# A six-layer block on one core: gate and output products tied behind the steps of a chunk loop, products grouped by tile shape, and router work moved

## The chip, the cores and the metric

The kernel runs on one core of a Trainium2 chip. The metric is the device time of one execution in microseconds (us); the time before is the median of three runs. Five engines work side by side, each through its own instructions in order: TensorE (PE) for matrix products, VectorE (DVE), ScalarE (ACT), GpSimd (POOL), and SyncE (SP), which here issues the DMA transfers. An engine waits on semaphores that the others, or landed transfers, raise.

## The reference

512 tokens of width 1024 in fp32 pass four layers (convolution, state-space, RWKV, convolution) and then two layers of another block, each a mixer of four parts and a mixture of experts.

```python
for i in range(4):                          # first block
    y = (short_conv, s5, rwkv7, short_conv)[i](x, ...)
    r = DN_ALPHA * x + y
    r = r + (p[i] @ ple_proj[i]) * sigmoid(r @ ple_gate[i])
    x = layer_norm(r, ln_g[i], ln_b[i])
...
def rwkv7_mixer(x, ...):                    # 16 heads of 64
    r, k, v, z = einsum("nbld,nde->nble", xs[:4], w_rkvz)
    ...
    sa = einsum("bhvk,bhk->bhv", state, -kk_t)          # each token t
    state = state * w_t + sa * (kk_t * a_t) + v_t * k_t
    out_t = einsum("bhvk,bhk->bhv", state, r_t)
    out = group_norm(out) * lnx_g + lnx_b + bonus
    return (out * silu(z)) @ w_out
...
# second block, layer l = 0, 1: s, b, g come from c @ w_ada
h = rms_norm(x, norm1_g[l]) * (1 + s1) + b1
x = x + g1 * token_mixer(h, ...)            # attention, pooling, HGRN recurrence, convolution
h = rms_norm(x, norm2_g[l]) * (1 + s2) + b2
x = x + g2 * hierarchical_moe(h, router weights, ...)   # 32 experts, two per token
```

## The kernel before

Activations are kept transposed: eight tiles `xp` of 128 channels by 512 tokens. A dense product takes its weights by `L338` (an SP load of raw weights `wr`), splits them into a high half `wh` on ACT (L315) and a low half `wl` on DVE (L317), and makes three products on PE (L423): high by high, low by high and high by low. The kernel is written with tile pools, and a scheduler that models time orders each engine's instructions before they are compiled. `behind(ins)` adds to that order one edge: what is issued under it comes after `ins` on the engine of `ins`. It adds no wait at run time.

**The RWKV chain** (`rwkv_chain`) goes through eight chunks of 64 tokens, 16 heads as 8 by 2 (`order`). Each chunk has four groups of products: `p1` (L1476, 16 products with `gx`), `p2` (L1481, 16 with `ad` and `rh`), `p3` (L1488, 16 with `bt`, for the next state `nsv`) and `po` (32: L1504 on `gx` and the state `sv`, L1502 on `ad` and `sa`), with ACT and DVE copies between them. `invert` (L1447, L1454, with DVE's L1456) makes the next chunk's `ad`; `loads` fetches it (L1431, L1432, L1433, L1436, L1438, L1325). At eight places in a chunk `fill()` advances generators: `zgen`, the gate's dense products `ptp<-xs` in pieces of six, then `wout(0)`, the first half of the output's products (`ptp<-H`, 256 columns); and `norms` and `post`, which normalise the chunks (`settle`, L1387) and gate them. Nothing but the scheduler's model sets where among the steps PE does these. What is left of them is done behind the chain.

**The state-space layer** makes y (L970 with `ow` and `X`, 64x64; L968 with `tw` and `U`, 128x64) in eight blocks. **The recurrence** of the second block's mixers makes its output from `At` and `v`, and `St` and `qb`, in four blocks (two layers by two).

**Bounds and router.** `bounds()` runs at the beginning of the first mixer, called mix0. Among its loads it stores two columns of `gs` (norm gain times scale) and of `mod` of each layer into DRAM (`d_gp`, [128, 8] turned to "k p", so in pieces of one value) and reads them back in another layout (`gp`, L1595), which the first mixture of experts uses. The stores of `mod` were placed by the scheduler in the last convolution layer, those of `gs` at the start of mix0. The seam into mix0 also holds the normalisation `mixer_operand` (L1671 sums squares on POOL and DVE, L458 reduces them on PE). `moe_before(l)` loads the router's weights (L2198), scales them by `gs` into `gw` on DVE (L2200), and makes the bias `rb` (L2199, L2203 on PE, L2204). It is written in the mixer behind its operands; the scheduler placed its load and `gw` in the seam. SP's loads go out on one DMA queue, in SP's order; an instruction that waits holds those behind it.

## Time and profile before

| | us |
|---|---|
| median of three runs | 3395.87 |
| the three runs | 3387.91, 3395.87, 3414.22 |
| profiled execution | 3395.55 |
| its span in the trace | 3393.8 |
| PE busy in it | 3023.4 |

The profile is one profiled execution. Its span is the trace's length; the profiled execution's own time holds some two microseconds more. A line of a timeline gives start, duration, engine, line, operation, output and inputs, shape and count, and in brackets the idle time of the engine ahead of it and what ended that. PE's records overlap, since products are pipelined, so the time of a run is the distance from its start to the next start. In the RWKV chain each small product leaves two records (x32 is 16 products). PEld is the load of the fixed operand, which runs beside PE.

### The profile page before, as it was taken

How to read it: one execution, taken by the hardware profiler on the slowest of the kernel's cores; microseconds unless marked ns; L12 is line 12 of the kernel's file. 1: busy time of each engine (PE TensorE's matmuls, PEld its weight loads, DVE VectorE, ACT ScalarE, POOL GpSimd, SP SyncE). 2: the span in 40 equal slices, each digit the busy share in tenths (PEclk: the TensorE clock that was granted, in tenths of full speed). 3: DMA queues.
4: the chain of work that ended last, by engine and by line, in shares of the span. 5: the costliest groups of instructions: out<-in, count | busy, mean ns of one | idle time of the engine just before them, and what ended most of it. 6: DMA issues, size and time to landing. Idle time of an engine off the chain costs nothing. (4 is left out here: it accounts for less than half of the span.)

```text
span 3393.8 us, 57476 instructions
## 1 busy us (share of the span) xinstructions
PE 3023.4 (89%) x23218; PEld 2174.3 (64%) x23218; DVE 2006.5 (59%) x3911; ACT 1031.5 (30%) x1695; POOL 876.2 (26%) x738
## 2 busy tenths in 40 slices
PE   6999989988879887998699979989979996998997
PEld 5677767865557776777575656555647565655564
DVE  6754495467965678788667454544447845354443
ACT  3233324356533332222253322111125343111111
POOL 2911321125422455420305230110011523010000
PEclk9999899988887897999798779999989887999999
DMA  5453562314677545586420048999982003799997
GB/s 168 133 158 100 147 173 67 110 59 140 177 198 222 169 150 167 162 235 211 90 75 20 28 159 323 413 415 415 416 303 67 28 17 152 295 414 407 416 416 323
DMA packets 443070, 690.46 MB, mean 203 GB/s; under 512 B 68720, under 2 KB 354800, under 8 KB 408944
## 3 DMA queue, kind: packets, MB, share of 16 engines
q1 hardware_dynamic: 441648, 684.63, 58.1%
q8 instruction: 185, 3.03, 0.4%
q10 hardware_dynamic: 1152, 2.10, 0.2%
q14 instruction: 85, 0.70, 0.1%
HBM read 642.08 MB, written 46.94 MB: 203 GB/s over the span
## 5 line engine op out<-in xcount | busy, mean ns | idle before, releaser
L317 DVE TENSOR_TENSOR wl<-wr,wh 128x1024 fp32r<-128x1024 f32 (+2 forms) x275 | 324.5, 1182 | 216.8 <-ACT wh L315 98.2
L315 ACT ACTIVATE wh<-wr 128x1024 fp32r<-128x1024 f32 (+2 forms) x290 | 270.7, 939 | 542.9 <-PE pmm L423 193.8
L2400 PE MATMUL pmm<-raw,xg 128*32 128x128 f32 (+1 forms) x5120 | 348.6, 323 | 5.0 <-DMA raw<-in_w_dram 4.1
L2400 PEld LDWEIGHTS pmm<-raw,xg 128*32 128x32 f32 (+1 forms) x5120 | 226.7, 123 | 121.8 <-issue 49.5
L2545 POOL TENSOR_SCALAR Ra<-sp,cf 128x512 f32<-128x512 f32 x28 | 44.6, 1593 | 789.0 <-PE pst L2584 739.1
L423 PE MATMUL pmm<-H,wh 128*128 128x512 f32 x680 | 206.8, 414 | 9.2 <-ACT cg L2073 4.0
L423 PE MATMUL pmm<-H,wl 128*128 128x512 f32 x680 | 204.3, 408 | 2.0 <-DVE wl L317 2.0
L423 PE MATMUL pmm<-L,wh 128*128 128x512 f32 x680 | 202.4, 406 | 0.1
L2560 DVE SCALAR_TENSOR_TENSOR xp<-pst,mod,xp 128x512 f32<-128x512 f32 x196 | 142.7, 747 | 64.1 <-PE pst L2585 60.0
L2427 PE MATMUL pas<-raw,gT 128*32 128x256 f32 (+1 forms) x1472 | 165.9, 450 | 12.1 <-DVE gT L2421 11.0
L1556 DVE SCALAR_TENSOR_TENSOR war<-wa,cs,war 128x256 f32<-128x256 f32 x252 | 156.6, 637 | 3.8
L423 PEld LDWEIGHTS pmm<-H,wh 128*128 128x128 f32 x680 | 130.6, 197 | 41.7 <-ACT cg L2073 4.2
L423 PEld LDWEIGHTS pmm<-H,wl 128*128 128x128 f32 x680 | 131.5, 196 | 34.8 <-issue 3.6
L423 PEld LDWEIGHTS pmm<-L,wh 128*128 128x128 f32 x680 | 131.1, 195 | 30.6 <-issue 1.7
L2635 ACT COPY Y<-pas 32x256 f32<-32x256 f32 (+1 forms) x92 | 37.8, 411 | 288.0 <-DVE Y L2635 287.9
L2453 PE MATMUL pst<-R,hH 128*128 128x320 f32 (+4 forms) x448 | 91.9, 321 | 33.3 <-DVE R L2444 30.3
L2407 DVE TENSOR_TENSOR g<-g,pmm 128x256 f32<-128x256 f32 (+1 forms) x56 | 20.3, 362 | 167.1 <-ACT g L2406 166.8
L2427 PEld LDWEIGHTS pas<-raw,gT 128*32 128x32 f32 (+1 forms) x1472 | 59.4, 119 | 91.7 <-issue 57.9
L2635 DVE COPY Y<-pas 32x256 f32<-32x256 f32 (+1 forms) x92 | 43.7, 475 | 125.8 <-PE pas L2427 118.1
L2406 ACT ACTIVATE g<-pmm 128x256 f32<-128x256 f32 (+1 forms) x56 | 18.9, 338 | 301.1 <-PE pmm L2400 301.1
L2400 PE MATMUL pas<-raw,xg 128*32 128x128 f32 (+1 forms) x2048 | 97.3, 292 | 11.7 <-SPq L2505 6.6
L2453 PEld LDWEIGHTS pst<-R,hH 128*128 128x128 f32 x448 | 69.4, 201 | 55.2 <-DVE R L2444 35.5
(869 smaller groups left out, 6801.2 us busy)
## 6 DMA issues: line engine op xcount, KB each, us to landing
raw<-in_w_dram SPq DMA_DIRECT2D x384, 1024.0 KB, 13.4
wa<-in_w_ada_dram SPq DMA_DIRECT2D x48, 1024.0 KB, 6.6
wr<-in_conv_w_in_dram SPq DMA_DIRECT2D x64, 512.0 KB, 4.8
wr<-in_w_in_dram SPq DMA_DIRECT2D x34, 512.0 KB, 4.1
wr<-in_ple_gate_dram SPq DMA_DIRECT2D x16, 1024.0 KB, 5.4
wr<-in_rwkv_w_rkvz_dram SPq DMA_DIRECT2D x16, 1024.0 KB, 5.4
wr<-in_conv_w_out_dram SPq DMA_DIRECT2D x8, 1024.0 KB, 5.2
wr<-in_ssm_w_in_dram SPq DMA_DIRECT2D x8, 1024.0 KB, 6.2
```

The costliest lines, as they stand in the source:

```text
L315: self.nc.scalar.activation(h, x, AF.Copy)
L317: (eng or self.nc.vector).tensor_tensor(l, x, h.bitcast(FT), OP.subtract)
L423: nc.tensor.matmul(ps[i], ws[i][w][:, perm[k]], x[k], start=n == first[i], stop=n == last[i])
L1556: E.scalar_tensor_tensor(acc, w[:, k], cs[:, k:k + 1], acc, op0=OP.mult, op1=OP.add)
L2400: nc.tensor.matmul(p[c * n:c * n + n, w // 2 * W:w // 2 * W + W], x[:, j, o:o + n], ws[w][:, jj, c * W:c * W + W], start=j == 0, stop=j == 7)
L2406: nc.scalar.activation(g, p[:, 0:W], AF.Sigmoid)
L2407: nc.vector.tensor_tensor(g, g, p[:, 0:W], OP.mult)
L2427: nc.tensor.matmul(py[q * n:q * n + n, 0:W], gT[:, o:o + n], ws[4 + j // 2][:, j % 2, q * W:q * W + W], start=j == 0, stop=j == 3)
L2453: T.matmul(p[:, :n], (self.hH, self.hL)[i // 4][:, i % 4, j], R[:, i % 4, :n], start=i == 0, stop=i == 7)
L2545: G.tensor_scalar(a, P[0], s, None, op0=OP.is_equal)
L2560: self.done = self.nc.vector.scalar_tensor_tensor(self.xp[m], p, self.mod[l][:, 40 + m:41 + m], self.xp[m], op0=OP.mult, op1=OP.add).ins
L2635: (nc.scalar.copy if q % 2 else nc.vector.tensor_copy)(self.block[1][o:o + n, q * W:q * W + W], p[q * n:q * n + n])
```

## The change

Six parts. In the chain, `fill(step)` issues the dense generators (`main`) behind the last product of the step just issued, so that on PE the piece comes after that step; the gate's pieces have three products, not six; four of the gate's output tiles are made ahead of the chain; and `po` makes its 16 products of one shape, then the 16 of the other. In the state-space layer and in the recurrence the two shapes of products are grouped in the same manner. The `d_gp` stores move from `bounds()` into `moe_before(0)`, and the `gp` load to the beginning of the mixture of experts. `moe_before` is issued behind the end of the mixer's normalisation (on DVE) and behind the last weight load (on SP).

```diff
-        self.nc.sync.dma_start(raw, W[:, c0:c0 + n].rearrange("(k p) n -> p k n", p=128))
+        self.loaded = self.nc.sync.dma_start(raw, W[:, c0:c0 + n].rearrange("(k p) n -> p k n", p=128)).ins
...
-                for gg in range(4):
-                    for c in range(3):
+
+                for c in range(3):
+                    for gg in range(4):
                         for g2, r in enumerate(rs):
                             o = py[g2][r, gg * 128:(gg + 1) * 128]
                             if c == 2:
-                                nc.tensor.matmul(o, U[q][:, m % 2 * 8 + g2 * 4 + gg], tw[g2][:, gg], start=False, stop=True)
+                                nc.tensor.matmul(o, U[q][:, m % 2 * 8 + g2 * 4 + gg], tw[g2][:, gg], start=False, stop=gg == 3)
...
-        zgen = self.dense_gen(zop, A["rwkv_w_rkvz"][0][3], range(0, D, 256), z_sink, ptag="tp", piece=6,
+        zgen = self.dense_gen(zop, A["rwkv_w_rkvz"][0][3], range(0, D, 256), z_sink, ptag="tp", piece=3,
                               then=(A["rwkv_w_out"][0], 0, 256))
...
-        def fill(n=1):
-            for _ in range(n):
+        def fill(step=None):
+
+            with self.behind(step and step.ins):
                 while main and next(main[0], StopIteration) is StopIteration:
                     main.pop(0)
-                for q in (norms, norms, post):
-                    if q and next(q[0], StopIteration) is StopIteration:
-                        q.pop(0)
+            for q in (norms, norms, post):
+                if q and next(q[0], StopIteration) is StopIteration:
+                    q.pop(0)
...
         nxt = loads(0)
+
+        while len(zs) < 4:
+            fill()
         for _ in invert(nxt[1], nxt[4]):
             fill()
...
-            fill()
+            fill(step)
...
-            for h in range(8):
-                for w in range(2):
-                    for q in range(2):
-                        rd = slice(64 - q * 64, 128 - q * 64)
-                        out = po[vr[q], h * 64:h * 64 + 64]
-                        if w:
-                            T.matmul(out, ad[sr[q], h, rd], sa[q][sr[q], h], start=False, stop=True)
-                        else:
-                            T.matmul(out, gx[:, q * 8 + h, rd], sv[q][:, h], start=True, stop=False)
+
+            for w in range(2):
+                for h, q in order:
+                    rd = slice(64 - q * 64, 128 - q * 64)
+                    out = po[vr[q], h * 64:h * 64 + 64]
+                    if w:
+                        step = T.matmul(out, ad[sr[q], h, rd], sa[q][sr[q], h], start=False, stop=h == 7)
+                    else:
+                        T.matmul(out, gx[:, q * 8 + h, rd], sv[q][:, h], start=h == 0, stop=False)
...
-        d = self.dr.tile([2, 2, 8, 128], FT, name="d_gp")
-        for l in range(2):
-            nc.sync.dma_start(d[l, 0].rearrange("k p -> p k"), self.gs[l][:, 8:16])
-            nc.sync.dma_start(d[l, 1].rearrange("k p -> p k"), self.mod[l][:, 24:32])
-        nc.sync.dma_start(self.gp, d.rearrange("l i (a b) c -> l i (a b c)", a=1).rearrange("l i (p j) -> p l i j", j=8))
...
-                for c in range(4):
-                    for hh, r in enumerate(half):
-                        o = po[r, c * 128:c * 128 + 128]
-                        T.matmul(o, vt[:, c, r], At[:, c * 4 + i * 2 + hh], start=True, stop=c == 0)
-                        if c:
-                            T.matmul(o, St[r, i * 3 + c - 1], qb[i][r, c * 128:c * 128 + 128], start=False, stop=True)
+
+                for w in range(2):
+                    for c in range(w, 4):
+                        for hh, r in enumerate(half):
...
-            self.moe_before(l)
+
+            with self.behind(normed), self.behind(self.loaded):
+                self.moe_before(l)
...
+        if self.d_gp is None:
+
+            self.d_gp = d = self.dr.tile([2, 2, 8, 128], FT, name="d_gp")
+            for i in range(2):
+                nc.sync.dma_start(d[i, 0].rearrange("k p -> p k"), self.gs[i][:, 8:16])
+                nc.sync.dma_start(d[i, 1].rearrange("k p -> p k"), self.mod[i][:, 24:32])
...
+        if not l:
+            nc.sync.dma_start(self.gp, self.d_gp.rearrange("l i (a b) c -> l i (a b c)", a=1).rearrange("l i (p j) -> p l i j", j=8))
```

PE in the RWKV chain before, at the third chunk, from the end of a gate piece to the beginning of `po` (the third column is output and inputs, then the shape and a count of equal rows):

```order
L423 MATMUL ptp_8845<-xs_7588,wh_8846 128x512
L423 MATMUL ptp_8845<-xs_7587,wl_8847 128x512
L1454 MATMUL pst_8156<-ad_7946,R_8126 32x32 x16
L1481 MATMUL pmm_8247<-rh_8223,ad_7946 64x64
L1504 MATMUL pmm_8301<-sv_7962,gx_7948 64x64
L1504 MATMUL pmm_8301<-sv_7963,gx_7948 64x64
L1481 MATMUL pmm_8247<-rh_8223,ad_7946 64x64 x15
L1488 MATMUL pas_8272<-sa_7950,bt_7949 64x64
L1502 MATMUL pmm_8301<-sa_7950,ad_7946 64x64
L1488 MATMUL pas_8272<-sa_7951,bt_7949 64x64
```

and the changed kernel at the second chunk, where `p1` has become L1481, `p2` L1486 and the two kinds of `po` L1509 and L1507:

```order
L1481 MATMUL pas_8078<-sv_7861,gx_7846 64x64
L423 MATMUL ptp_7817<-xs_7573,wl_7819 128x512
L423 MATMUL ptp_7817<-xs_7580,wl_7819 128x512
L423 MATMUL ptp_7817<-xs_7587,wl_7819 128x512
L1486 MATMUL pmm_8103<-rh_8079,ad_7844 64x64 x16
L423 MATMUL ptp_8122<-xs_7538,wh_8123 128x512
L423 MATMUL ptp_8122<-xs_7545,wh_8123 128x512
L423 MATMUL ptp_8122<-xs_7552,wh_8123 128x512
L1509 MATMUL pmm_8153<-sv_7860,gx_7846 64x64
L1509 MATMUL pmm_8153<-sv_7861,gx_7846 64x64
```

Gate pieces of three now stand behind `p1` and behind `p2`, and the L1509 products that begin here are sixteen in a row.

SP at the start of mix0 before, from the stores of `gs` to the router's loads:

```order
L1593 DMA d_gp<-gs_13250 128x8x1
L1593 DMA d_gp<-gs_13253 128x8x1
L1651 DMA cf_13402<-in_constf_dram 128x1499
L1653 DMA mi_13404<-in_consti_dram 128x192
...
L338 DMA wr_13486<-in_w_in_dram 128x8x128
L2198 DMA wr_15246<-in_w_router_dram 128x8x36
L2199 DMA rb_15248<-in_rb_dram 128x36
```

and the changed kernel in the middle of mix0, from the mixer's last input weights to the first of its output weights:

```order
L338 DMA wr_14833<-in_w_in_dram 128x8x128
L2205 DMA d_gp<-gs_13250 128x8x1
L2206 DMA d_gp<-mod_78 128x8x1
L2205 DMA d_gp<-gs_13253 128x8x1
L2206 DMA d_gp<-mod_79 128x8x1
L2209 DMA wr_15245<-in_w_router_dram 128x8x36
L2210 DMA rb_15247<-in_rb_dram 128x36
L2477 DMA gp<-d_gp 128x4x8
L338 DMA wr_15493<-in_w_out_dram 128x4x256
```

The four stores have come together, ahead of the router's weights.

DVE in the seam into mix0 before, with the router's `gw` ahead of the sum of squares:

```order
L517 SCALAR_TENSOR_TENSOR xp_76<-xp_76,vec,pst_13191 128x512
L517 SCALAR_TENSOR_TENSOR xp_77<-xp_77,vec,pst_13191 128x512
L2200 TENSOR_TENSOR gw_15247<-wr_15246,gs_13250 128x288
L1671 TENSOR_TENSOR sq_13276<-sq_13276,sq_13281 128x512
L1671 TENSOR_TENSOR sq_13296<-sq_13296,sq_13298 128x512
```

and in the changed kernel, in the middle of mix0 (`hd` belongs to the recurrence, `mq` to attention):

```order
L1815 TENSOR_TENSOR hd_14187<-hd_14187,hq_13912 128x8x32
L1815 TENSOR_TENSOR hd_14242<-hd_14242,hq_13836 128x16x16
L2211 TENSOR_TENSOR gw_15246<-wr_15245,gs_13250 128x288
L2018 SCALAR_TENSOR_TENSOR mq_13683<-mq_13683,vec_13393,pas_13901 128x512
L2018 SCALAR_TENSOR_TENSOR mq_13706<-mq_13706,vec_13393,pas_13916 128x512
L1810 TENSOR_TENSOR hd_14303<-hb_13747 128x16x16
L1811 TENSOR_TENSOR hd_14303<-hb_13747 128x16x16
L317 TENSOR_TENSOR wl_14592<-wr_14346,wh_14591 128x1024
```

`gw` has moved from the seam to a place between `hd` and `mq` (there L2018, before L2015).

## Rows read from the trace of the kernel before

**Rows 1.** The page's busy time, share of the span and instructions: TensorE.

```profile
PE 3023.4 (89%) x23218; PEld 2174.3 (64%) x23218; DVE 2006.5 (59%) x3911; ACT 1031.5 (30%) x1695; POOL 876.2 (26%) x738
```

**Rows 2.** Windows of the chain: busy time by engine, granted clock, DMA share, GB/s.

```profile
1040.00:1060.00 20.00, 18.24 (x277) 14.40 (x277) 12.54 (x27) 7.68 (x14) 9.09 (x7) 1.00 0.89 283
1060.00:1080.00 20.00, 17.92 (x252) 14.58 (x248) 11.74 (x39) 4.55 (x10) 4.16 (x4) 0.50 0.81 235
...
1100.00:1120.00 20.00, 18.91 (x218) 15.81 (x218) 11.51 (x25) 6.84 (x16) 14.82 (x20) 0.55 0.62 171
1120.00:1140.00 20.00, 19.43 (x326) 16.85 (x326) 14.26 (x40) 8.84 (x15) 4.57 (x5) 1.00 0.63 161
...
1160.00:1180.00 20.00, 12.47 (x99) 10.38 (x98) 10.82 (x33) 7.73 (x16) 7.38 (x14) 0.81 0.46 144
```

**Rows 3.** Timeline of TensorE in the chain, 1055 to 1131.

```profile
1055.86 0.63 PE L423 MATMUL ptp<-xs,wh 128*128 128x512 f32 x2
...
1059.11 0.29 PE L1481 MATMUL pmm<-rh,ad 64*64 64x64 f32 x2 [1.76 <-DVE ad L1456]
...
1068.80 0.48 PE L1504 MATMUL pmm<-sv,gx 128*64 128x64 f32 x4
...
1072.09 1.06 PE L1447 MATMUL pst<-t,ad 32*32 32x32 f32 x32
1073.08 1.98 PE L1476 MATMUL pas<-sv,gx 128*64 128x64 f32 x32
...
1111.73 0.58 PE L423 MATMUL ptp<-H,wh 128*128 128x256 f32 x1
...
1125.54 0.34 PE L1504 MATMUL pmm<-sv,gx 128*64 128x64 f32 x4
...
1129.23 0.69 PE L1454 MATMUL pst<-ad,R 32*32 32x32 f32 x32
1129.85 1.15 PE L1476 MATMUL pas<-sv,gx 128*64 128x64 f32 x32
1130.93 0.38 PE L423 MATMUL ptp<-H,wh 128*128 128x256 f32 x1
```

**Rows 4.** Timeline of the seam into mix0, all engines.

```profile
1653.94 1.28 POOL L1671 TENSOR_TENSOR sq<-sq,sq 128x512 f32<-128x512 f32 x1
...
1670.60 0.46 DVE L2200 TENSOR_TENSOR gw<-wr,gs 128x288 f32<-128x288 f32 x1 [16.31 <-DMA wr<-in_w_router_dram]
1670.97 1.28 DVE L1671 TENSOR_TENSOR sq<-sq,sq 128x512 f32<-128x512 f32 x2
...
1671.81 0.34 PE L458 MATMUL ptp<-ones,sq 128*128 128x1 f32 x1 [23.35 <-DVE sq L1671]
```

**Rows 5.** DMA issues, 1630 to 1680: count, KB each, median us to landing.

```profile
mi<-in_consti_dram SPq DMA_DIRECT2D x1, 96.0 KB, 22.7
...
d_gp<-gs SPq DMA_DIRECT2D x2, 4.0 KB, 18.7
```

**Rows 6.** The tile `d_gp`: its four stores and one load, to landing.

```profile
DMA to landing us min/median/max: 6.2/12.0/20.2
```

**Rows 7.** Timeline of mix0, 1777 to 1786: SP, DVE, TensorE.

```profile
1777.27 0.37 SPq L338 DMA_DIRECT2D wr<-in_w_in_dram  x1
...
1781.19 0.52 DVE L1815 TENSOR_TENSOR hd<-hd,hq 128x256 f32<-128x256 f32 x1 [0.36 <-ACT hd L1812]
...
1782.81 1.61 DVE L2015 SCALAR_TENSOR_TENSOR mq<-mq,vec,pas 128x512 f32<-128x512 f32 x2 [1.10 <-PE pas L2013]
...
1785.34 1.12 PE L2013 MATMUL pas<-me,cf 8*128 8x512 f32 x2
```

**Rows 8.** A window of mix0; columns as in rows 2.

```profile
1831.00:1851.00 20.00, 18.21 (x155) 9.76 (x153) 19.89 (x40) 4.84 (x13) 11.81 (x11) 0.68 0.01 2
```

**Rows 9.** Timeline of TensorE in the state-space layer, 504.9 to 505.5.

```profile
504.99 0.27 PE L970 MATMUL pas<-ow,X 64*64 64x128 f32 x1
...
505.10 0.27 PE L970 MATMUL pas<-ow,X 64*64 64x128 f32 x1
...
505.31 0.32 PE L968 MATMUL pas<-tw,U 128*64 128x128 f32 x1
```

More of the change, by code (lines that the diff above doesn't have):

```diff
@@ L967, in ssm_layer @@
                             if c == 2:
-                                nc.tensor.matmul(o, U[q][:, m % 2 * 8 + g2 * 4 + gg], tw[g2][:, gg], start=False, stop=True)
+                                nc.tensor.matmul(o, U[q][:, m % 2 * 8 + g2 * 4 + gg], tw[g2][:, gg], start=False, stop=gg == 3)
                             else:
-                                nc.tensor.matmul(o, X[r, m * 4 + gg, c, 0:64], ow[gg // 2][r, gg % 2, c], start=c == 0, stop=False)
+                                nc.tensor.matmul(o, X[r, m * 4 + gg, c, 0:64], ow[gg // 2][r, gg % 2, c], start=c + gg == 0, stop=False)
                 yt = self.wt("yt", (128, 8, 4, 16), tag="w", bufs=self.NW)
@@ L1475, in rwkv_chain @@
             for h, q in order:
-                T.matmul(p1[sr[q], h * 64:h * 64 + 64], gx[:, q * 8 + h, q * 64:q * 64 + 64], sv[q][:, h], start=True, stop=True)
+                step = T.matmul(p1[sr[q], h * 64:h * 64 + 64], gx[:, q * 8 + h, q * 64:q * 64 + 64], sv[q][:, h], start=True, stop=True)
             ACT.activation(flat(rh), p1, AF.Copy, scale=-1.0)
-            fill()
+            fill(step)
             p2 = self.pt()
             for h, q in order:
-                T.matmul(p2[sr[q], h * 64:h * 64 + 64], ad[sr[q], h, q * 64:q * 64 + 64], rh[sr[q], h], start=True, stop=True)
+                step = T.matmul(p2[sr[q], h * 64:h * 64 + 64], ad[sr[q], h, q * 64:q * 64 + 64], rh[sr[q], h], start=True, stop=True)
             for q in range(2):
                 (ACT.copy if q else V.tensor_copy)(flat(sa[q][sr[q]]), p2[sr[q]])
-            fill()
+            fill(step)
             if nsv is not None:
@@ L1487, in rwkv_chain @@
                 for h, q in order:
-                    T.matmul(p3[sr[q], h * 64:h * 64 + 64], bt[:, q * 8 + h], sa[q][:, h], start=True, stop=True)
+                    step = T.matmul(p3[sr[q], h * 64:h * 64 + 64], bt[:, q * 8 + h], sa[q][:, h], start=True, stop=True)
                 for q in range(2):
                     V.tensor_tensor(flat(nsv[q][sr[q]]), p3[sr[q]], flat(dec[sr[q]]), OP.add)
-            fill()
+            fill(step)
             while len(norms) > 1:
@@ L1495, in rwkv_chain @@
             po = self.pt()
-            for h in range(8):
-                for w in range(2):
-                    for q in range(2):
-                        rd = slice(64 - q * 64, 128 - q * 64)
-                        out = po[vr[q], h * 64:h * 64 + 64]
-                        if w:
-                            T.matmul(out, ad[sr[q], h, rd], sa[q][sr[q], h], start=False, stop=True)
-                        else:
-                            T.matmul(out, gx[:, q * 8 + h, rd], sv[q][:, h], start=True, stop=False)
+            for w in range(2):
[6 more added lines that the diff above has]
+                        T.matmul(out, gx[:, q * 8 + h, rd], sv[q][:, h], start=h == 0, stop=False)
             ACT.activation(flat(o), po, AF.Copy)
             norms.append(settle(c, o))
-            fill()
+            fill(step)
             for s in range(2):
@@ L1510, in rwkv_chain @@
                     next(inv, None)
-                fill()
+                fill(step)
             sv = nsv
@@ L1590, in bounds @@
         self.gp = self.c2.tile([128, 2, 2, 8], FT, name="gp")
-        d = self.dr.tile([2, 2, 8, 128], FT, name="d_gp")
-        for l in range(2):
-            nc.sync.dma_start(d[l, 0].rearrange("k p -> p k"), self.gs[l][:, 8:16])
-            nc.sync.dma_start(d[l, 1].rearrange("k p -> p k"), self.mod[l][:, 24:32])
-        nc.sync.dma_start(self.gp, d.rearrange("l i (a b) c -> l i (a b c)", a=1).rearrange("l i (p j) -> p l i j", j=8))
-    lb = None
+    lb = d_gp = None
     def lower_bounds(self):
@@ L1718, in mixer @@
         op = self.mixer_operand(l)
+        normed = self.done
         if self.vec2 is None:
@@ L1896, in hgrn @@
                 po = self.pt("st", bufs=2)
-                for c in range(4):
-                    for hh, r in enumerate(half):
-                        o = po[r, c * 128:c * 128 + 128]
-                        T.matmul(o, vt[:, c, r], At[:, c * 4 + i * 2 + hh], start=True, stop=c == 0)
-                        if c:
-                            T.matmul(o, St[r, i * 3 + c - 1], qb[i][r, c * 128:c * 128 + 128], start=False, stop=True)
+                for w in range(2):
+                    for c in range(w, 4):
+                        for hh, r in enumerate(half):
+                            o = po[r, c * 128:c * 128 + 128]
+                            if w:
+                                T.matmul(o, St[r, i * 3 + c - 1], qb[i][r, c * 128:c * 128 + 128], start=False, stop=c == 3)
+                            else:
+                                T.matmul(o, vt[:, c, r], At[:, c * 4 + i * 2 + hh], start=c == 0, stop=False)
                 o = self.at("ho")
```

## The prediction

> **What bounds the kernel now.** I read the page's busy times first: TensorE (PE) is busy for 3023 of 3394 us [rows 1]. So time comes back only where PE idles, where its clock is low, or where a product takes it longer than it has to. I therefore read one by one the stages that the change touches: the RWKV chain in windows and then as a timeline, the seam in front of mix0 with its DMA issues, and the stretch of mix0 to which the router's work moves.
>
> In the chain PE is busy for 17 to 19 of 20 us, but its granted clock is 1.00 up to 1060, then 0.50, 0.55 in the window from 1100, and 1.00 again from 1120 [rows 2]: it falls from 2.4 to 1.2 GHz. The timeline has products of the gate (L423, `ptp<-xs`) among the chunk steps up to 1056, and no large product more until those of the output begin at 1111.73 [rows 3]. The low clock covers nearly that gap. The same rows show the price of changing tile shape: the products of `po`, which alternate two of 64x64 (L1502) with two of 128x64 (L1504), take from 1125.54 to 1129.23 for 14 such pairs, 0.264 us each, while the 16 products of one shape at 1129.85 last until the next start at 1130.93, 0.135 a pair. At the low clock eight pairs take 3.29 us (1068.80 to 1072.09), 0.41 each. Once PE waits 1.76 us for DVE's inverse.
>
> In the seam PE waits 23.35 us for DVE's sum of squares, and DVE itself stood 16.31 us at `gw` for the router's weights [rows 4]. POOL had made the sum's last input by 1655.2. The DMA list tells why the weights came late: the 96 KB table `mi`, issued right behind the two 4 KB stores `d_gp<-gs`, took 22.7 us to land, and the stores 18.7 in the median [rows 5]; the later one took 20.2, a store alone 12.0 [rows 6]. These stores hold up what stands behind them.
>
> **The change part by part.** **The chain.** It issues the same products, but between its start and its last `po` product PE's order changes tile shape 119 times where it did 215 times. A whole chunk's `po` goes from 16 x 0.264 = 4.2 to 16 x 0.135 = 2.2 us for 15 changes fewer or so: 0.13 a change. The pieces between steps bring changes of their own, so the net count is what matters: 96 x 0.13 = 12.5 us less.
>
> The gate's pieces now last to chunk 5. If the clock then stays up, the 50 us or so in which PE is busy between 1060 and 1115 shrink: a pair of `po` costs 0.41 low and 0.264 full (1.55 times), a run of 16 is 1.98 low and 1.15 full by its records (1.72 times); with 1.65, 50 x (1 - 1/1.65) = 20 us. Chunk 6 has no pieces in the new order, so I leave one chunk low and take 14. The ends: 0, if the clock falls for another reason, and 20. PE's idle time is 5.5 us in the four windows shown from 1040 to 1140; pieces now stand where it waits, so 4 of it and its like goes (0 to 7). The chain starts up to 3 us later, as the bonus's loads now stand ahead of it: 1 us. That is -12.5 - 14 - 4 + 1, about **-30** (-8 to -42). Some 38 of the output's products leave the chain and are done behind it, where PE idles 7.5 us of 1160 to 1180 [rows 2], which hides them. One of them occupies PE at most 0.38 us by its record [rows 3]: without that cover, 14 us at most, and perhaps 5.
>
> What is late next there is the chunk's loads. They moved 235 to 283 GB/s in the busiest windows [rows 2], and a chain shorter by a fifth asks for about a fifth more than its mean; the 283 shows that this can be had. DVE is busy for 11 to 14 of 20 us, so it has room.
>
> **The shapes in the state-space layer and the recurrence.** Two products of one shape start 0.11 us apart, one after a change of shape 0.21 [rows 9]: 0.10 a change. Each of the eight blocks of y loses six of its eight: 8 x 6 x 0.10 = **-5** (-2 to -7, since the first block has other products in it). The recurrence's four blocks lose 13 each, at most 5 us by the same price; other products stand among them, so **-2** (0 to -5).
>
> **The seam.** With `gw` gone, DVE's sum can start at 1655.3 instead of 1670.97 [rows 4]: **-15.5** (-10 to -17). The stores leave the queue there too, so no other load takes the wait's place: what stood behind them lands some 20 us sooner. The stores of the other two columns leave the third conv layer, where PE waits little: **-1** (0 to -3). In the second layer `gw` leaves a seam too; I take nothing for it, 0 to -2.
>
> **Where the router's work goes.** This is the dear part. All four stores now stand on SP in a row behind the last input weights, issued at 1777.27 [rows 7], and the router's weights right behind them. `gw` stands in DVE's order between the two `hd` products that ended at 1781.7 and the `mq` products, which ran at 1782.81. Two stores took 20.2 us together, so four take 40; the weights, 2 us behind, land at about 1820. DVE stands 38 us, and behind it `mq`, the low halves of the last weights and every `hd` of the recurrence. PE can go on to the third product of L2013, which needs the buffer that `mq` empties and ran at 1785.34: it loses 34 us. ACT and POOL can run ahead a little, so 2 comes back; from 1831 DVE is busy 19.89 of 20 us [rows 8], so no more than that. After an idle stretch the clock starts low, as in 1160 to 1180 (0.81) [rows 2]: 1 us. Together **+33** (+24 to +45; the lower end if four stores share the engines better than two did, the upper if each takes 12 us as one alone). Behind the stores SP also holds `gp` and the output's weights, which are wanted only 100 us later and cost nothing.
>
> The sum, on the profiled execution's own 3395.55 us (the median of the runs is 3395.87, the same): -30 - 5 - 2 - 15.5 - 1 + 33 = -20.5, so **3375 us**.
>
> **The rivals.** **The stores hold nobody.** The router's weights pass them, and only the gains remain: 3375 - 33 = 3342. Against it stands `mi`, 96 KB that did not pass two of them [rows 5]. For it: the columns have long been ready, and the queue is nearly empty in this stretch of mix0, where the seam had several loads at once. The Trainium skill ("DMA: Bandwidth & Descriptors", section Queues, rings and completion order) says that each DMA engine consumes descriptors in ring order, but that completion is not first in, first out for an issuing engine, since a copy may use fewer of the rings. By its second half the weights could pass, and this rival's 3342 would be the time; the 22.7 us of `mi` agree with its first half.
>
> **The clock stays low.** If it falls for the small products themselves rather than for the missing large ones, the 14 us and the 4 of idle time don't come back: 3375 + 18 = 3393. For it: pieces of three products are short beside runs of 16. Against: with pieces among the steps the clock was 1.00 up to 1060 [rows 2].
>
> **The ties make PE wait.** This one ends slower. PE takes its products in order, so a piece tied behind a step, whose weights are not split yet or whose PSUM buffer ACT and DVE have not emptied, stops the next step too; before, the next step went ahead. There are some 64 such places in the chain, so the saving of 30 us is gone from 30/64 = 0.47 us at each. If three places a chunk waited as long as PE's wait at 1059.11 [rows 3], it would be 24 x 1.76 = 42 us: 3375 + 42 = 3417. Against it: the last gate weights are loaded ahead of chunk 0's blocks, and DVE has room.
>
> **How the numbers follow.** The forecast gets 0.55 (its own range 3357 to 3394), stores that hold nobody 0.20 (3330 to 3355), the low clock 0.15 (3385 to 3402), ties that wait 0.10 (3400 to 3440). A range that leaves out half of the second and most of the last reaches from 3343 to 3402. One per cent is 34 us, about what this kernel's runs (3387.91 to 3414.22) can tell from no change: faster than 3362 has 0.27 (nearly all of the second case and the low tail of the first), slower than 3430 has 0.06, and 0.67 lies between.
>
> **What the profile after would show.** Right: no `gw` in the seam, and PE's wait for the sum of squares there down to 7 or 8 us; one idle time of DVE of 35 to 40 us, with the router's weights as its releaser, between `hd` and `mq`; the last of the four stores landing some 40 us after its issue; `po` in runs of 16 products of about 1.1 us; clock 1.00 through chunks 0 to 5 and lower only near chunk 6; a chain of 120 to 130 us where it was 155. Wrong: the router's weights landing within 10 us; idle time ahead of L423 in the chain; a clock of 0.5 with pieces in place; PE's waits in the chain ended by loads of `gx`.

## The result and the profile after

The changed kernel takes 3351.56 us in the median of four runs (3343.26 to 3362.5), the kernel before 3397.12 in the same comparison; the ratio is 0.9854, with a 95% interval from 0.9832 to 0.9876. That is some 45 to 50 us less, where 20.5 were forecast. The profiled execution took 3351.78 us, its span is 3350.0. TensorE's busy time fell from 3023.4 us [rows 1] by 44, the whole of the span's loss:

```profile
PE 2979.4 (89%) x23218; PEld 2154.2 (64%) x23218; DVE 2016.2 (60%) x3911; ACT 1032.3 (31%) x1696; POOL 882.7 (26%) x738
```

To see where the time went I paired every TensorE instruction of the one trace with the same one of the other (its source line, tiles and count) and took the median difference of their starts in stretches of 20 us. The sum so far is that difference, called the shift below:

```
place (us, trace of before)       sum so far   this place   forecast
state-space layer, to 540             -4.9        -6.7         -5
up to the chain's start, 1000         +2.2        +7.1         +1 (in the chain's term)
the RWKV chain, to 1160              -22.3       -24.5        -31
its tail, the third conv layer, 1640 -33.6       -11.3         -1
seam into mix0, 1660                 -49.5       -15.9        -15.5
mix0 up to gw, 1760                  -50.6        -1.1          0
gw, 1780                             -30.3       +20.3        +33
to the recurrence's output, 1900     -29.4        +0.9          0
the recurrence's output, 1920        -43.9       -14.6         -2 (both layers)
to the experts, 2040                 -41.2        +2.7          0
the rest, to the end of the span     -43.8        -2.6          0
```

The first row starts from +1.8, the difference that the two executions had before any edit.

**The chain.** It ran from 1009.38 to 1137.28 (127.9 us, where it took 155.2). These are windows of it, columns as in [rows 2]:

```profile
1020.00:1040.00 20.00, 19.27 (x351) 14.65 (x349) 11.32 (x30) 6.74 (x13) 5.14 (x5) 1.00 0.96 269
1040.00:1060.00 20.00, 17.55 (x292) 13.45 (x294) 13.11 (x37) 8.24 (x17) 4.05 (x4) 0.91 0.86 245
1060.00:1080.00 20.00, 20.00 (x410) 15.81 (x407) 13.89 (x46) 7.28 (x14) 3.64 (x4) 1.00 0.80 225
1080.00:1100.00 20.00, 15.78 (x283) 12.55 (x279) 15.67 (x31) 8.46 (x19) 15.21 (x21) 0.91 0.87 278
1100.00:1120.00 20.00, 17.23 (x264) 15.31 (x265) 14.43 (x37) 8.50 (x18) 14.15 (x23) 0.74 0.45 113
```

The granted clock stays at 0.91 to 1.00 up to 1100 and dips behind it, at chunk 6, to 0.74; over the whole chain it is 0.91 where it was 0.80. In the timeline of TensorE a `po` run of one shape takes 1.15 us, so some 2.3 for the two runs of a chunk, against 4.2 for a mixed `po` [rows 3]:

```profile
1009.38 0.22 PE L1449 MATMUL pst<-t,ad 32*32 32x32 f32 x2 [1.25 <-DMA t<-d_t]
...
1136.13 1.15 PE L1507 MATMUL pas<-sa,ad 64*64 64x64 f32 x32
```

TensorE's waits in the chain (us in total, times, longest) are 10.7 us in all before and 14.5 in the changed kernel. These are the largest of each:

```profile
PE pmm L1481 <- DVE ad L1456: 3.9, 3, 1.8
```

```profile
PE pst L1449 <- DMA t<-d_t: 4.7, 5, 1.3
```

**The seam.** DVE's sum no longer stands behind `gw`. TensorE waits 7.44 us for it, where it waited 23.35 [rows 4]:

```profile
1620.58 2.95 DVE L1670 TENSOR_TENSOR sq<-sq,sq 128x512 f32<-128x512 f32 x3
...
1622.28 3.55 PE L458 MATMUL ptp<-ones,sq 128*128 128x1 f32 x16 [7.44 <-DVE sq L1670]
```

**The router's new place.** The timeline of mix0 (SP, DVE, TensorE):

```profile
1726.81 0.95 SPq L2205 DMA_DIRECT2D d_gp<-gs  x1
...
1731.02 1.20 SPq L2209 DMA_DIRECT2D wr<-in_w_router_dram  x1
...
1749.48 0.37 SPq L2477 DMA_DIRECT2D gp<-d_gp  x1
1749.82 0.46 DVE L2211 TENSOR_TENSOR gw<-wr,gs 128x288 f32<-128x288 f32 x1 [18.75 <-DMA wr<-in_w_router_dram]
1750.20 1.40 DVE L2018 SCALAR_TENSOR_TENSOR mq<-mq,vec,pas 128x512 f32<-128x512 f32 x2
1750.99 2.07 PE L2016 MATMUL pas<-me,cf 8*128 8x512 f32 x2 [16.21 <-DVE mq L2018]
```

The wait is there, between `hd` and `mq`, and TensorE's third L2016 waits for it, as forecast; but it is 18.75 us and not 38. All four stores had landed at 1749.5, 22.7 us behind the issue of the first, and none took more than 19.0 us from its own issue:

```profile
DMA to landing us min/median/max: 2.1/16.2/19.0
```

**The recurrence.** This is the place that I had nearly passed over. In the kernel before, its output products in mix0 take from 1907.70 to 1925.36, with four products of L423 among them. Each product leaves two records (x2), and the shape changes at nearly every product:

```profile
1907.70 1.11 PE L1900 MATMUL pst<-hA,hvt 128*64 128x128 f32 x6
...
1910.75 0.69 PE L1902 MATMUL pst<-hqb,hS 64*64 64x128 f32 x2
1911.37 0.69 PE L1900 MATMUL pst<-hA,hvt 128*64 128x128 f32 x2
...
1924.75 0.69 PE L1902 MATMUL pst<-hqb,hS 64*64 64x128 f32 x2
1925.36 2.07 PE L423 MATMUL pmm<-H,wh 128*128 128x512 f32 x4
```

The granted clock was low all the while (a window, columns as in [rows 2]):

```profile
1907.00:1925.00 18.00, 18.00 (x63) 9.54 (x64) 4.88 (x19) 2.23 (x4) 0.00 (x0) 0.50 0.09 29
```

In the changed kernel the same 28 products take 5.06 us:

```profile
1876.40 1.97 PE L1905 MATMUL pst<-hA,hvt 128*64 128x128 f32 x16
1878.31 1.40 PE L1903 MATMUL pst<-hqb,hS 64*64 64x128 f32 x12
1879.64 1.09 PE L1905 MATMUL pst<-hA,hvt 128*64 128x128 f32 x16
1880.66 0.87 PE L1903 MATMUL pst<-hqb,hS 64*64 64x128 f32 x12
1881.46 2.05 PE L464 MATMUL pas<-ident,lr 128*128 128x128 f32 x16
```

### The profile page after: what moved, and what is told of

Its sections match the earlier page's. It is cut to its first block, busy times and chain, and to the rows that moved or that the text cites. A ratio compares the mean times of both kernels' runs of the same rounds, so it can differ in the third digit from the quotient of the medians.

```text
span 3350.0 us, 57495 instructions
## 1 busy us (share of the span) xinstructions
PE 2979.4 (89%) x23218; PEld 2154.2 (64%) x23218; DVE 2016.2 (60%) x3911; ACT 1032.3 (31%) x1696; POOL 882.7 (26%) x738
## 5 line engine op out<-in xcount | busy, mean ns | idle before, releaser
L423 PE MATMUL pmm<-H,wh 128*128 128x512 f32 x680 | 205.7, 412 | 12.2 <-ACT wh L315 8.2
L423 PE MATMUL pmm<-L,wh 128*128 128x512 f32 x680 | 203.1, 406 | 3.7 <-DVE L L317 2.2
L423 PE MATMUL pmm<-H,wl 128*128 128x512 f32 x680 | 202.3, 405 | 1.5 <-DVE wl L317 1.5
L423 PEld LDWEIGHTS pmm<-H,wh 128*128 128x128 f32 x680 | 130.6, 197 | 45.0 <-ACT wh L315 9.9
L423 PEld LDWEIGHTS pmm<-L,wh 128*128 128x128 f32 x680 | 130.7, 194 | 37.0 <-DVE L L317 4.1
L423 PEld LDWEIGHTS pmm<-H,wl 128*128 128x128 f32 x680 | 131.4, 195 | 33.7 <-DVE wl L317 2.4
L2418 DVE TENSOR_TENSOR g<-g,pmm 128x256 f32<-128x256 f32 (+1 forms) x56 | 20.3, 363 | 162.3 <-ACT g L2417 162.0
```

The lines of the kernel that those rows point to most:

```text
L423: nc.tensor.matmul(ps[i], ws[i][w][:, perm[k]], x[k], start=n == first[i], stop=n == last[i])
L2418: nc.vector.tensor_tensor(g, g, p[:, 0:W], OP.mult)
```

## Experiments

Times are medians; ratios are to the kernel before in the same session, with 95% intervals; the sessions ran on several chips. "Chain" is the time from the first product of the first inverse to the end of the last `po`; "recurrence" is from the first of its output products to the end of the last, in mix0 and mix1. The last three columns are each from one profile.

```
kernel                        ratio                    chain   recurrence   wait at the first gw
before                        1                        155.2   17.7, 17.3   16.31 (in the seam)
changed                       0.9854 (0.9832-0.9876)   127.9    5.1,  5.3   18.75
recurrence mixed              0.9874 (0.9838-0.9909)   128.9   17.7, 11.8   16.15
router's loads first          0.9820 (0.9794-0.9846)   125.2    6.5,  5.2    4.05
untied                        0.9889 (0.9860-0.9918)   127.8    6.3,  5.9   15.33
po mixed                      0.9914 (0.9886-0.9942)   136.3    6.2,  6.3   15.59
eight stores                  0.9855 (0.9823-0.9888)   124.7    6.2,  5.4   28.50
two stores (gs, gs)           0.9859 (0.9827-0.9891)   125.3    6.5,  5.6   19.07
recurrence alone              0.9972 (0.9944-1.0000)   153.7    5.3,  5.2   13.78 (in the seam)
no tiles ahead                0.9899 (0.9871-0.9928)   126.1    5.8,  5.3    2.65
chain alone                   0.9938 (0.9911-0.9964)   125.1   17.7, 17.7   12.94 (in the seam)
router alone                  1.0013 (0.9993-1.0033)   160.7   17.4, 17.3   16.31 (in mix0)
stores in bounds              0.9815 (0.9788-0.9843)   128.3    6.4,  5.3    1.51
one store                     0.9856 (0.9821-0.9892)   125.8    5.5,  5.2    9.22
two of mod (one run)          -                        123.6    6.5,  5.3   16.24
two of layer 0 (one run)      -                        125.2    6.4,  5.7   10.28
y alone                       0.9983 (0.9962-1.0005)   155.5   11.8, 17.2   14.83 (in the seam)
stores in bounds, again       0.9861 (0.9830-0.9891)   128.6    6.4,  5.6    1.39
changed, again                0.9875 (0.9853-0.9897)   126.0    6.4,  5.3   16.83
router's loads first, again   0.9811 (0.9790-0.9831)   128.2    5.5,  5.4    3.31
```

**The recurrence's products mixed again**, in the changed kernel.

```diff
-                for w in range(2):
-                    for c in range(w, 4):
-                        for hh, r in enumerate(half):
+                for c in range(4):
+                    for hh, r in enumerate(half):
```

> The changed kernel with the recurrence's products in their old order, the two shapes alternating. Theory: grouping them is where the unforeseen gain came from; the trace has 17.7 us for them in mix0 before and 5.1 after, and some 6 us of the same kind in mix1, so this kernel is 15 to 20 us slower than the changed one (about 3369). Rival: the 12 us there came from the granted clock (0.55 in that window before, 0.88 after), which other parts of the change set, and the grouping is worth the 2 to 5 us that I had priced: 3353 to 3357, with a high clock in that stretch.

It took 3359.28 us, between what theory and rival say, and its ratio can't be told from the changed kernel's. The trace settles it (its execution, 3368.73 us, was the slowest of the four): in mix0 the products are back at 17.7 us, and everything behind is 12.9 us later than in the changed kernel. So the grouping is the cause and not another part of the change. The clock has a share of its own: it is 0.50 in the window of exactly these products in mix0, while in mix1 the same alternation ran at 0.86 and took 11.8 us, 0.36 us a product where it was 0.62. These are the window in mix0 and the timeline in mix1:

```profile
1877.00:1896.00 19.00, 19.00 (x66) 10.21 (x67) 5.11 (x21) 2.90 (x6) 0.00 (x0) 0.50 0.09 28
```

```profile
2747.29 0.43 PE L1900 MATMUL pst<-hA,hvt 128*64 128x128 f32 x2
2747.66 0.43 PE L1902 MATMUL pst<-hqb,hS 64*64 64x128 f32 x2
```

**The recurrence grouped, alone**, in the kernel before (the same diff the other way).

> The kernel before with the recurrence's products grouped by shape and nothing else. Theory: its 17.7 and 17.3 us in the two layers become 5 to 6.5 each, on the path in both, so 20 to 24 us less: a ratio of 0.993 to 0.994. Rival: in the second layer other work takes the freed time, as the shift of the changed kernel against the one before grew there by only 6 us: 13 to 18 us, 0.995 to 0.996.

17.7 and 17.3 us became 5.3 and 5.2, but the ratio says 9 us (0 to 19) and not 24. By the shifts mix0 gives 10.5 us. In mix1 the products end 13 us earlier, of which 5 are taken back at once: TensorE then waits 2.89 us for ACT's split of the next weights and works the first of them at the low clock. What else is missing there was lost ahead of the recurrence, where the schedule of mix1 came out 5.7 us longer. So the rival is nearer, with an even smaller number. The products' own loss, 12 us in each layer, is what the whole change shows too.

**The router's loads ahead of the four stores.**

```diff
+        nc.sync.dma_start(wr, self.A["w_router"][l].rearrange("(k p) n -> p k n", p=128))
+        nc.sync.dma_start(self.rb, self.A["rb"][l])
         if self.d_gp is None:
 ...
-        nc.sync.dma_start(wr, self.A["w_router"][l].rearrange("(k p) n -> p k n", p=128))
-        nc.sync.dma_start(self.rb, self.A["rb"][l])
```

> The changed kernel with the four stores issued behind the router's two loads instead of ahead of them. Theory: the stores held the router's weights; with the loads first these land within 3 to 6 us, DVE's idle time of 18.75 us at gw is gone, and so are PE's 16 us: 3333 to 3339. Rival: the stores then hold the bias or the output's weights and a wait of the same size appears further on, or gw waits nearly as long for another reason: 3348 to 3354.

It took 3337.79 us, as the theory had it, and the wait at `gw` is 4.05 us:

```profile
1729.03 0.46 DVE L2211 TENSOR_TENSOR gw<-wr,gs 128x288 f32<-128x288 f32 x1 [4.05 <-DMA wr<-in_w_router_dram]
```

By the shifts it gains 17 to 18 us on the changed kernel there and gives back 5 to 7 up to the experts, in pieces of 2 or 3. No single wait took the place.

**Without the ties.**

```diff
-            with self.behind(step and step.ins):
+            with self.behind(None):
```

> The changed kernel without the ties: fill issues the dense pieces with no edge behind the step; pieces of three, the first four gate tiles ahead of the chain and the grouped output products stay. Theory: the ties keep large products among the steps to chunk 5 and with them the clock; without them the pieces run out earlier, a stretch of the chain falls to 1.2 GHz, and it is 10 to 15 us longer: 3362 to 3367. Rival: the gain of the chain is that of the grouping alone, and this kernel is within 4 us of the changed one.

3355.34 us and a chain of 127.8: the rival. The clock falls to 0.76 and 0.67 from 1060 to 1100 here, where the changed kernel has 1.00 and 0.91; but over the whole chain it is 0.89 against 0.91, the chain is not longer, and by the shifts the profile is as long as the changed kernel's.

```profile
1060.00:1080.00 20.00, 15.17 (x286) 13.02 (x288) 11.29 (x36) 6.92 (x16) 6.90 (x9) 0.76 0.70 202
1080.00:1100.00 20.00, 16.47 (x228) 14.38 (x225) 11.86 (x29) 6.09 (x14) 15.02 (x20) 0.67 0.70 212
```

**`po` in its old order**, the ties kept.

```diff
-            for w in range(2):
-                for h, q in order:
+            for h in range(8):
+                for w in range(2):
+                    for q in range(2):
```

> The changed kernel with the chunk's output products in their old order, two of 64x64 and two of 128x64 in turn; the ties stay. Theory: each of the eight chunks pays 2 us more at the full clock, so the chain is 14 to 17 us longer: 3365 to 3369. Rival: the longer products fill time in which PE now waits for loads, DVE and ACT, and half of it or more is hidden: 3352 to 3359.

3368.13 us. The chain is 136.3, only 8.4 us longer than with the groups, and TensorE's waits in it fell to 6.7 us where the changed kernel has 14.5: half of the 16 us is hidden under waits that are there anyway, which is the rival's mechanism. The time is the theory's all the same: by the shifts some 10 us come in the chain and 13 in mix1, where this edit changes nothing, so that agreement is luck.

**The chain's part alone, and the router's alone**, in the kernel before: of the diff of the change, the hunks of `rwkv_chain`, and those with these lines.

```diff
+            with self.behind(normed), self.behind(self.loaded):
+                self.moe_before(l)
...
+        if self.d_gp is None:
```

> The kernel before with the part of the change in the RWKV chain alone: ties, pieces of three, four gate tiles ahead, grouped output products. Theory: the chain takes 125 to 128 us where it took 155, starts some 5 us later, and the layers behind keep what is left: 20 to 25 us less, a ratio of 0.9926 to 0.9941. Rival: a part of it is given back behind the chain, where more of the output's products are left: 10 to 15 us, 0.9956 to 0.997.

> The kernel before with the router's part alone, as in the change: stores and router loads behind the mixer's last input weights, gw out of the seam. Theory: 16 us less in the seam and 18 to 21 us more at gw, and nothing else: a ratio of 0.999 to 1.002. Rival: the stores also cost something in the third conv layer and in the seam beside gw, so that their leaving brings 8 to 10 us more: 0.996 to 0.9985.

The chain gives 21 us (12 to 30), as the theory had it. The router's part gives nothing, its theory too: 15.9 us less in the seam by the shifts, 17.8 more at `gw`, a ratio of 1.0013.

**The y products alone**, in the kernel before.

```diff
-                for gg in range(4):
-                    for c in range(3):
+                for c in range(3):
+                    for gg in range(4):
```

> The kernel before with the y products of the state-space layer grouped by shape and nothing else. Theory: 6 to 7 us less in that stage and 1 or 2 given back behind it: a ratio of 0.998 to 0.9987. Rival: the parts measured alone sum to 32 us against 44 to 50 of the whole, and what is missing lies here: 0.995 or less.

0.9983, 6 us less (13 less to 2 more): the theory, though the interval holds no change too. The four parts alone sum to 32 us less (21, 9.5 and 6 less, 4.4 more), where the whole is 42 to 50 less in two sessions. Each part is uncertain by 7 to 9 us, so this may be chance; it is not settled.

**Eight stores**, four of them into a second tile, all ahead of the router's loads; **two of gs**, **one**, **two of mod**, and the **two of layer 0** ahead, the others behind.

```diff
+            e = self.dr.tile([2, 2, 8, 128], FT, name="d_gq")
+            for i in range(2):
+                nc.sync.dma_start(e[i, 0].rearrange("k p -> p k"), self.gs[i][:, 8:16])
+                nc.sync.dma_start(e[i, 1].rearrange("k p -> p k"), self.mod[i][:, 24:32])
```

and, for the two of `gs` (the others are built alike),

```diff
             for i in range(2):
                 nc.sync.dma_start(d[i, 0].rearrange("k p -> p k"), self.gs[i][:, 8:16])
-                nc.sync.dma_start(d[i, 1].rearrange("k p -> p k"), self.mod[i][:, 24:32])
...
         nc.sync.dma_start(self.rb, self.A["rb"][l])
+        if first:
+            for i in range(2):
+                nc.sync.dma_start(d[i, 1].rearrange("k p -> p k"), self.mod[i][:, 24:32])
```

> The changed kernel with four more stores of the same columns, into a second DRAM tile, behind the first four and ahead of the router's loads. Theory: a store costs what its 1024 single values cost, some 5 us (four landed within 22 us of the first issue), so DVE's idle time at gw grows from 18.75 to about 40 us and the time to about 3371. Rival: what counts is that the queue is choked at all; two stores took 20.2 us and four took 19.0, so eight take the same, and the time stays within 5 us of the changed kernel's.

> The changed kernel with the two stores of gs ahead of the router's loads and the two of mod behind them. Theory (about 5 us a store): DVE's idle time at gw is 8 to 11 us, the time 3342 to 3346. Rival: these two are the very pair that took 20.2 us in the old seam, and take it again: idle time of 16 us or more, the time that of the changed kernel.

> The changed kernel with one of the four stores ahead of the router's loads and three behind. Theory: one store chokes the queue for 9 to 12 us, as one alone did in the conv layer, so DVE waits 6 to 10 us at gw: 3340 to 3346. Rival: the three stores behind slow the loads ahead of them too, and the wait is the 16 to 19 us of two and of four: 3348 to 3354.

> The changed kernel with the two stores of mod ahead of the router's loads and those of gs behind. Theory: the price is that of the number of stores up to two (9 us for one, 18 for two, no more for four), whichever they are: DVE waits 15 to 19 us at the first gw. Rival: only the stores of gs choke the queue behind them, as one, two and four stores with one, two and two of gs in them would also say: the wait is under 6 us.

> The changed kernel with the stores of gs and mod of the first layer ahead of the router's loads and those of the second behind. Theory (number of stores): 15 to 19 us of waiting at the first gw. Rival (stores of gs alone): 7 to 11 us, as with one store.

The waits at `gw`, in the order eight, two of `gs`, one, two of `mod`, two of layer 0:

```profile
1756.68 0.46 DVE L2215 TENSOR_TENSOR gw<-wr,gs 128x288 f32<-128x288 f32 x1 [28.50 <-DMA wr<-in_w_router_dram]
```

```profile
1741.71 0.46 DVE L2214 TENSOR_TENSOR gw<-wr,gs 128x288 f32<-128x288 f32 x1 [19.07 <-DMA wr<-in_w_router_dram]
```

```profile
1735.80 0.46 DVE L2214 TENSOR_TENSOR gw<-wr,gs 128x288 f32<-128x288 f32 x1 [9.22 <-DMA wr<-in_w_router_dram]
```

```profile
1741.36 0.46 DVE L2214 TENSOR_TENSOR gw<-wr,gs 128x288 f32<-128x288 f32 x1 [16.24 <-DMA wr<-in_w_router_dram]
```

```profile
1729.22 0.46 DVE L2214 TENSOR_TENSOR gw<-wr,gs 128x288 f32<-128x288 f32 x1 [10.28 <-DMA wr<-in_w_router_dram]
```

Neither the number of stores nor the tile that they read sets the wait, so the expectation that goes by the number failed at the two stores of layer 0, and the one that goes by `gs` at the two of `mod`. The two of `gs` wait as their rival has it, and eight stores came out between theory and rival. One store costs 9.2 us and the two of one layer 10.3; the two of one kind, one from each layer, cost 16.2 or 19.1, and all four 15.3 to 18.75 in six profiles. From its issue the router's load took 11.5 us behind one store and behind the two of one layer, 17.1 and 20.4 behind one of each layer, 16.1 to 18.8 behind four, and 6.2 and 6.9 with the stores behind it. So the wait goes by layers: the second store of a layer adds about 1 us, the second layer 5 to 9. This rule was read out of these runs, with one profile each, and no run was made to test it. A layer's two stores write 4 KB stretches of DRAM that lie side by side, those of one kind 8 KB apart; whether that is the reason, no run here shows. The 28.5 us of eight stores are of another make: SP issued the router's load only 19.7 us behind the first store, where 4.2 lie between them in the changed kernel, and it landed 16.4 us later.

```profile
1720.54 0.58 SPq L2205 DMA_DIRECT2D d_gp<-gs  x1
...
1740.22 3.77 SPq L2213 DMA_DIRECT2D wr<-in_w_router_dram  x1
```

The eight left the kernel's time where it was, 3347.66 us; its schedule of mix0 is another one, and what it lost at `gw` came back within 100 us by the shifts. The time of one store, 3342.23 us, is its theory's, but its ratio of 0.9856 is the changed kernel's.

**No gate tiles ahead of the chain**, with the router's loads first.

```diff
-        while len(zs) < 4:
-            fill()
```

> The kernel with the router's loads first, and without the four gate tiles ahead of the chain, so that all of the gate's pieces go among the steps. Theory: the chain's loads no longer stand behind the bonus's, the chain starts 2 to 5 us earlier, more pieces than places make it last no longer: 3333 to 3337. Rival: the gate is done later, and with it the output's first half and the tail behind the chain: 3340 to 3345.

3360.37 us, worse than either said. The view of waits on TensorE shows the mistake in both: the first inverse product goes out early, but then TensorE stands 31.8 us for the chunk's `t`, a time that the four tiles had filled, and the work left out there stands behind the chain.

```profile
PE pst L1449 <- DMA t<-d_t: 34.6, 3, 31.8
PE pst L1388 <- POOL ot L1383: 9.5, 3, 6.7
```

**The stores back in bounds, the router's work left in its new place.**

```diff
         self.gp = self.c2.tile([128, 2, 2, 8], FT, name="gp")
+        self.d_gp = d = self.dr.tile([2, 2, 8, 128], FT, name="d_gp")
+        for i in range(2):
+            nc.sync.dma_start(d[i, 0].rearrange("k p -> p k"), self.gs[i][:, 8:16])
+            nc.sync.dma_start(d[i, 1].rearrange("k p -> p k"), self.mod[i][:, 24:32])
...
-        if self.d_gp is None:
...
```

> The changed kernel with the four stores back where they were (issued by bounds, so two in the third conv layer and two at the start of mix0); the router's loads and gw stay behind the last input weights. Theory: the seam waited for gw alone, so it keeps its 16 us, and no store stands ahead of the router's weights: 3333 to 3340, as with the router's loads first. Rival: the tables and weights behind the two stores in the seam are late, and mix0's start waits for them instead: 3345 to 3353.

> The kernel with the stores back in bounds and the router's work behind the last input weights, once more with more rounds: 0.980 to 0.983 of the kernel before if it is 16 us faster than the changed kernel; 0.985 if what it showed was chance.

3332.56 us in the first session and 3349.77 in the second, ratios of 0.9815 and 0.9861. Both traces agree on the places: 15.9 us less in the seam in the first, a wait of 1.51 and 1.39 us at `gw`; the 17 us between the two profiles are spread over the whole kernel. So the seam waited for `gw` alone. But the second ratio is the one that the expectation called chance, and the two sessions differ by as much as the edit is worth. Hence the last comparison, both kernels in one session, five runs each:

> The changed kernel again, beside the next kernel on the same chip. Theory: 0.983 to 0.988 of the kernel before, as when it was first timed.

> The kernel with the router's loads ahead of the four stores again. Theory: the wait at gw is on the path, so it is 12 to 18 us (0.004 to 0.005) below the changed kernel in the same rounds. Rival: the difference seen before was the chance of a session, and the two are within 5 us.

3350.61 us against 3327.36: 0.9875 and 0.9811, with intervals that don't touch.

```profile
1742.03 0.46 DVE L2211 TENSOR_TENSOR gw<-wr,gs 128x288 f32<-128x288 f32 x1 [16.83 <-DMA wr<-in_w_router_dram]
```

```profile
1726.28 0.46 DVE L2211 TENSOR_TENSOR gw<-wr,gs 128x288 f32<-128x288 f32 x1 [3.31 <-DMA wr<-in_w_router_dram]
```

The wait at `gw` is on the path: by the shifts 16 us of the 23 come there. The rest, with which the difference exceeds the theory's 12 to 18, is spread over other places. Beside the same baseline, the kernel with the router's loads first is 65 us below the kernel before.

## Why the prediction was wrong

The time lies in the range, but the forecast of less than one per cent doesn't hold. Two terms were mis-sized, and they add up: of the 25 us that the forecast is short, the stores make 12.7 and the recurrence 12.6. The other misses nearly cancel: the chain with its start brought 12.6 less than forecast, the stages behind it 10.3 more. The prediction has no reason for that, so it is luck.

- **"Two stores took 20.2 us together, so four take 40."** This step failed. The mechanism was right in each part: the stores hold the router's weights, DVE stands at `gw`, TensorE gets to the third product and no further. But the price doesn't grow with the number of stores: the four had landed 22.7 us behind the first one's issue, and the two of the old seam were one of each layer, which by the runs above is already the price of four. The term was +33 and measured +20.3, and the runs with fewer stores or none ahead show that it is the stores. The rival in which they hold nobody fell. Of the rule that the prediction cites from the Trainium skill ("DMA: Bandwidth & Descriptors", section Queues, rings and completion order), it is the half on the order in the rings that these 18.75 us agree with.
- **"The recurrence's four blocks lose 13 each, at most 5 us by the same price."** This step failed too, in its price. That of 0.10 us came from [rows 9], at the full clock. In the recurrence a product with a change of shape took 0.62 us at 1.2 GHz and one without 0.24 (eight in 1.91, 1876.40 to 1878.31), so about 0.38 a change; at the higher clock 0.36 against 0.13 (eight in 1.02), so 0.23. The rows of before that are shown above stood in the trace for the reading. The count was off the other way: with the next block's first product a block had 12 changes and keeps 2, so it loses 10. In mix0 the stretch lost 12.6 us: 2.0 are the four products of L423, which now stand elsewhere, some 7.6 are 20 changes at 0.38, and the rest is the clock, which rose to 1.00 within the grouped products (0.50 up to 1878.30, 1.00 from 1879.60). In mix1 it lost 12.0. Of that mix0 kept 14.6 - 2.7 = 11.9 up to the experts; mix1 gave 6 to 9 at its products by the shifts, but the stages just ahead of them had lost a part of that, so some 4 are left.
- **The chain.** Its forecast of -30 measured -27.3 in itself and -24.5 + 7.1 = -17.4 with its start, which came 4 to 7 us later in the profiles with this edit and not 1. By SP's order the bonus's loads stand ahead of the first inverse's tiles there; that they are the cause was not tried. The changes of shape fell as counted, and the clock rose from 0.80 to 0.91 over the chain. But the 4 us of idle time did not come back: TensorE's waits in the chain went from 10.7 us to 14.5 (9.6 with the chain's part alone), with the loads of `t` now the largest. The cause that I gave is only half right. The groups alone are worth 8.4 us beside the ties; the untied kernel has the same chain as the tied one, at nearly the same clock, so it is not the ties that bring the 14. Grouping and clock may each cover for the other; no run takes both away, so this is not shown, and neither is what the shorter pieces bring. The bounds of the terms add up to -9.5 and -39.5 and not to -8 and -42.
- **The seam**: forecast -15.5, -15.9 in every profile that has the edit.
- **State-space layer**: forecast -5, measured -6.7 by the shifts and 6 less with the part alone.
- **The tail and the third conv layer**: forecast -1, measured -11.3. With the chain alone it is there too (-25 to -35 between 1260 and 1640), so it comes with the chain's part and not with the stores' leaving. In before, the start of that layer has TensorE waiting 8.5 us for L598; after it, the waits are others. In nine profiles with the chain's edit or most of it that stretch brings from 2 to 13 us, so the number is uncertain, and I have no cause for it.
- **The rival that ends slower** (ties that make TensorE wait) fell: no wait ahead of L423 in the chain stands among the larger ones.

## What to carry to other kernels

A change of tile shape is not one price: read it where the alternation stands, at the clock that it has there, from the distance between starts of neighbouring rows. Before an edit moves a load behind something in a queue, ask whether the two need that order at all: here the swap of two blocks of lines was worth 23 us in one session, half of what the whole change brought, and 12 by the ratios of two other sessions. And work that fills a wait for loads is worth its place ahead of a loop, even if the loop then starts a little later.

## What the runs showed that I had not expected

Two stores of single values from one layer held the load behind them hardly longer than one, two from different layers did: 9.2 us for one, 10.3 for two of a layer, 16.2 and 19.1 for two of different layers, 15.3 to 18.75 for four. And TensorE's clock was low in the recurrence's output while TensorE was busy all through: 0.50 and 0.52 in the kernel before. Of the ten stretches of alternating shapes in five profiles eight were at 0.50 to 0.54 and two at 0.86, with the same instructions. In mix0 of the kernel before the clock was 0.50 already from 1905.00 to 1907.70, so there it fell ahead of these products, and the grouped ones of the changed kernel began at 0.50 too (1876.40 to 1878.30). What decides it stays open.
